# Seven products of a pair in another order, and the last chunk's output with tokens on the partitions

## The chip, the core and the metric

The kernel runs on one core of one Trainium2 chip. The metric is the time of one execution on the device in microseconds; given are the median and the single times. The profile is that of one execution, taken by the hardware profiler. Its engines are called PE (TensorE, matmuls; PEld are its weight loads), DVE (VectorE), ACT (ScalarE), POOL (GpSimd) and SP (SyncE, which issues all DMAs here).

## The reference

One decoder layer over a prompt of 4096 tokens of width 1024, and beside it over 8 single sample tokens, all in float32:

```
h = rmsnorm(x) @ w_in          # u_pool | z_pool | q | k | v | z_attn | g_pool | g_attn
pooled = trailing means of u_pool over 2/4/8/16 tokens, minus u_pool
att    = sliding-window (128) attention, 8 query heads, 2 kv heads, bias and sinks
br_pool = (pooled @ w_grp * pool_scale * silu(z_pool)) @ w_br_pool
br_attn = (att * silu(z_attn)) @ w_br_attn
x = x + (sigmoid(g_pool) * br_pool + sigmoid(g_attn) * br_attn) @ w_out
y = rmsnorm(x, g_final)
```

Outputs are y for prompt and samples, and the keys, values and pooling inputs of the last positions.

## The kernel before

**Numbers.** [...]

**Chunks.** The prompt is worked on in 8 chunks of 512 tokens; chunk 1 carries the 8 sample tokens too. Activations stand with channels on the partitions and tokens along the free dimension. For each chunk the order is: the k and v pair, two pairs of q, the z_attn pair; eight half-blocks, each of which does one pair of the projection and half a block of attention (scores, exponentials, transposes, product with v) in between; the rest of the gate pairs; eight `branch` steps (two products of 4 k-tiles over 512 columns, multiplied by the gates and summed into `mh` and `ml`); eight output steps with `w_out` (24 matmuls of 512 columns each, L938 adds the residual); and in the meantime the normalised input of the next chunk (`prep_sq`, `prep_rs`, `prep_xt`), written into `xt7`. The final norm of a chunk, `finish`, is done during the next chunk's first pairs; after the last chunk it stands alone at the end.

**Pairs.** Two output tiles of the projection (128 rows each) times 512 tokens over 1024 channels are done as a 2x2 block product in the Winograd form of Strassen's scheme: seven products of 4 k-tiles (12 matmuls of 256 columns), instead of eight. `xt7` holds seven combinations of the input, T_1 to T_4 and B_11, B_21, B_22. The weights s1 to s4 are sums of weight blocks, made in chunk 0, kept in DRAM split already, and loaded as 512 KB (L173); 11, 12 and 22 are plain blocks, loaded as 256 KB (L151) and split each time. The partial sums lie in two PSUM banks: Q holds the halves q6 and q1, R the halves r5 and r7. In chunk 1, with 260 columns, the four have a bank each. Products go into q6 (s2), q1 (11, then 12), r5 (s1, then s4), r7 (s3, then 22); between the rounds, copies and additions by ACT and DVE read the banks:

- L300 copies q1 into u2, L301 adds q6 to it
- L305 and L306 add r5 and r7 to u2 into q[3]
- L313 copies q1 into q[0] after product 12
- L317 (chunk 1: L320, L321) adds u2 to r5 and r7 after s4 and 22

A product that writes a bank waits until the readers of that bank are through. `part1` is the first four products, `part2` the other three; in the half-blocks attention stands between them. PSUM has five buffers for pairs, scores and other products together, two for transposes and small things, and one for the product with v.

**Order.** The program is written in the order above; a planner then puts each engine's instructions into one sequence by its own model of times, ready ones first, in the order of the program where several are ready. Each engine works through its sequence in order, and SP's sequence is the order of the DMAs. Weights have 8 split tiles (5 in chunk 0) and 4 raw tiles.

**The end of the last chunk.** Step 7 adds the residual (L938), ACT squares (L947), PE sums the squares over the channels for each token (L382, columns of one), DVE and POOL make 1/rms (L371, L373), PE spreads it over the partitions (L398), ACT copies it (L401), DVE and POOL multiply the eight tiles (L654, L652), and SP stores eight tiles of 256 KB (L657).

## Time and profile before

| what | value |
|---|---|
| median of 2 runs | 2419.95 us (2416.96 and 2422.94) |
| profiled execution | 2424.16 us, span 2422.4 us |
| PE busy | 2336.5 us, 96% |
| DVE busy | 1650.7 us, 68% |
| ACT busy | 1159.9 us, 48% |
| POOL busy | 309.4 us, 13% |
| DMA | 584.67 MB, mean 241 GB/s |

Rows that begin with two numbers are in order of time: start and length in microseconds, engine, line, operation, output and inputs, and in brackets how long the engine had been idle and what ended that. Rows of groups have the number of instructions behind x, then busy microseconds and mean nanoseconds of one, then the idle time before them. Rows of waits have who waited for whom, the total, how often, and the longest.

### The profile page before, as it was taken

To read this page: it belongs to the slowest core of one execution; us is meant where nothing else is said; L and a number is where in the kernel's file an instruction comes from. 1 tells how busy PE (TensorE), PEld (TensorE's weight loads), DVE (VectorE), ACT (ScalarE), POOL (GpSimd) and SP (SyncE) were. 2 spreads that over 40 slices of the span, in tenths; PEclk is the share of its full clock that TensorE was granted. 3 is DMA by queue.
4 is the path that set the end of the run, shared out by engine and by line. 5 is a ranking of instruction groups with operands and counts; after the bars stand their busy time and mean duration, and the time that the engine had idled before them with its cause. 6 is when DMAs were issued, how large, how long until landed. Compare 5 with 4: busy or idle time off the path is not lost.

```text
span 2422.4 us, 44090 instructions
## 1 busy us (share of the span) xinstructions
PE 2336.5 (96%) x16547; PEld 2174.9 (90%) x16547; DVE 1650.7 (68%) x3224; ACT 1159.9 (48%) x2359; POOL 309.4 (13%) x258
## 2 busy tenths in 40 slices
PE   7989999999999999999999999999999999999998
PEld 6979879999999988998889988899889998899986
DVE  7888886856768656676567855677556765668652
ACT  6667545554346633465235642456423663245531
POOL 0000002300024000330004200041001410023000
PEclk9989999999999999999999999999999999999999
DMA  6657878766886667867678667776677776687654
GB/s 215 222 183 252 283 274 305 221 231 235 275 296 237 232 227 244 287 234 238 216 254 280 233 232 233 258 275 227 226 236 270 252 239 220 227 290 244 213 195 144
DMA packets 236515, 584.67 MB, mean 241 GB/s; under 512 B 36828, under 2 KB 39165, under 8 KB 236301
## 3 DMA queue, kind: packets, MB, share of 16 engines
q1 hardware_dynamic: 236300, 581.85, 70.4%
q8 instruction: 131, 2.15, 0.4%
q14 instruction: 84, 0.68, 0.1%
HBM read 517.35 MB, written 64.40 MB: 240 GB/s over the span
## 4 chain that ended last, share of the span: by engine, by line
PE 69%; DVE 15%; DMA 8%; ACT 4%; issue 3%; SPq 0%; POOL 0%; DVEq 0%; ACTq 0%; POOLq 0%
PE hb L184 12%; PE hb L185 12%; PE hb L186 12%; PE mm L184 9%; PE mm L186 9%; PE mm L185 9%; DMA H<-in_xt 3%; DMA wr<-in_xq 2%; DVE w L139 2%; PE tp L521 2%; DMA wr<-in_wall 2%; PE pv L532 2%; DVE H L763 1%; DVE xt L189 1%; DVE oy L654 1%
## 5 line engine op out<-in xcount | busy, mean ns | idle before, releaser
L184 PE MATMUL hb<-xt,w 128*128 128x256 f32 x3312 | 938.7, 284 | 35.2 <-DVE H L306 22.7
L186 PE MATMUL hb<-xt,w 128*128 128x256 f32 x3312 | 931.1, 282 | 5.7 <-DVE w L139 5.6
L185 PE MATMUL hb<-xt,w 128*128 128x256 f32 x3312 | 933.4, 282 | 0.6 <-DVE xt L189 0.3
L184 PEld LDWEIGHTS hb<-xt,w 128*128 128x128 f32 x3312 | 626.5, 189 | 47.0 <-DVE H L306 27.7
L186 PEld LDWEIGHTS hb<-xt,w 128*128 128x128 f32 x3312 | 627.7, 190 | 8.0 <-DVE w L139 8.0
L185 PEld LDWEIGHTS hb<-xt,w 128*128 128x128 f32 x3312 | 626.4, 189 | 3.9 <-DVE xt L189 1.8
L138 ACT CAST w<-wr 128x512 fp32r<-128x512 f32 x586 | 359.2, 617 | 338.4 <-PE hb L186 205.2
L139 DVE TENSOR_TENSOR w<-wr,w 128x512 fp32r<-128x512 f32 x418 | 285.7, 689 | 150.3 <-ACT w L138 147.1
L139 POOL TENSOR_TENSOR w<-wr,w 128x512 fp32r<-128x512 f32 x168 | 253.3, 1510 | 479.7 <-ACT w L138 375.7
L184 PE MATMUL mm<-mh,w 128*128 128x512 f32 (+1 forms) x576 | 213.3, 371 | 1.4 <-ACT mh L898 1.4
L186 PE MATMUL mm<-mh,w 128*128 128x512 f32 (+1 forms) x576 | 213.0, 370 | 1.6 <-DVE w L139 1.6
L185 PE MATMUL mm<-ml,w 128*128 128x512 f32 (+1 forms) x576 | 212.1, 368 | 0.8 <-DVE ml L899 0.6
L373 POOL TENSOR_TENSOR rs<-rs,nhalf 128x4 f32<-128x4 f32 (+1 forms) x18 | 18.4, 1024 | 1341.1 <-DVE rs L371 1341.1
L891 DVE SCALAR_TENSOR_TENSOR H<-H,mm 128x512 f32<-128x512 f32 (+1 forms) x144 | 90.2, 627 | 108.4 <-PE mm L186 107.9
L502 ACT ACTIVATE LL<-LL,nm 128x257 f32<-128x257 f32 (+1 forms) x256 | 126.5, 497 | 68.3 <-DVE nm L499 68.2
L459 ACT CAST xt<-H 128x256 fp32r<-128x256 f32 (+6 forms) x92 | 63.1, 687 | 161.6 <-DVE H L448 111.3
L184 PE MATMUL mm<-xt,w 128*128 128x260 f32 x476 | 135.6, 285 | 0.9 <-ACT U L300 0.5
L185 PE MATMUL mm<-xt,w 128*128 128x260 f32 x476 | 134.7, 283 | 0.7 <-DVE xt L189 0.7
L186 PE MATMUL mm<-xt,w 128*128 128x260 f32 x476 | 134.4, 283 | 0.6 <-DVE w L139 0.3
L186 PEld LDWEIGHTS mm<-mh,w 128*128 128x128 f32 x576 | 108.1, 188 | 22.8 <-DVE w L139 2.5
L185 PEld LDWEIGHTS mm<-ml,w 128*128 128x128 f32 x576 | 108.2, 188 | 21.7 <-DVE ml L899 1.9
L184 PEld LDWEIGHTS mm<-mh,w 128*128 128x128 f32 x576 | 108.1, 188 | 21.0 <-ACT mh L898 1.9
(194 smaller groups left out, 4048.5 us busy)
## 6 DMA issues: line engine op xcount, KB each, us to landing
w<-ss SPq DMA_DIRECT2D x476, 512.0 KB
wr<-in_wall SPq DMA_DIRECT2D x597, 256.0 KB
w<-so SPq DMA_DIRECT2D x96, 512.0 KB
ss<-w SPq DMA_DIRECT2D x56, 512.0 KB
H<-in_xt SPq DMA_DIRECT2D x32, 512.0 KB
wr<-in_xq SPq DMA_DIRECT2D x56, 256.0 KB
H<-in_xt SPq DMA_DIRECT2D x56, 256.0 KB
out_y<-oy SPq DMA_DIRECT2D x28, 512.0 KB
```

What stands on the lines that cost most here:

```text
L138: nc.scalar.copy(w[:, 0], raw)
L139: (eng or nc.vector).tensor_tensor(out=w[:, 1], in0=raw, in1=w[:, 0].bitcast(F32), op=ALU.subtract)
L184: mm(ps, lhsT=w[:, 0, k0 + k, :], rhs=rh, start=start and k == 0, stop=False, **kw)
L185: mm(ps, lhsT=w[:, 0, k0 + k, :], rhs=rl, start=False, stop=False, **kw)
L186: mm(ps, lhsT=w[:, 1, k0 + k, :], rhs=rh, start=False, stop=stop and k == nk - 1, **kw)
L189: nc.vector.tensor_tensor(out=out, in0=a, in1=hi.bitcast(F32), op=ALU.subtract)
L459: nc.scalar.copy(hi[:, s_], x)
L502: nc.scalar.activation(out=L[:, j, k0:2 * P + 1], in_=L[:, j, k0:2 * P + 1], func=AF.Exp, bias=nm[:, j:j + 1], accum_out=den[:, j:j + 1])
L521: nc.tensor.transpose(tp[:, j, :], L[:, j, kb * P:(kb + 1) * P], ident)
L532: mm(pv, lhsT=vs[:, b + kb, g, :], rhs=pt[:, kb, m].rearrange("p j q -> p (j q)"), start=n == 0 and m == 0, stop=n == len(kbs) - 1 and m == 1)
L654: nc.vector.scalar_tensor_tensor(out=y, in0=y, scalar=gf[:, e:e + 1], in1=rsp[:, 0:n], op0=ALU.mult, op1=ALU.mult)
L891: nc.vector.scalar_tensor_tensor(out=t[:, a:b], in0=t[:, a:b], scalar=1.0, in1=ps, op0=ALU.add, op1=ALU.mult)
```

## The change

**The pair.** The order of the products becomes s1, s3 (bank R), s2, 11 (bank Q), s4, 22 (R), 12 (Q), in all chunks. After s3, ACT copies r5 into q[3] and DVE adds r7; after 11, u2 is made as before; after 22, q[3] gets u2 added, and then r5 and r7 get it as before; the copy of q1 into q[0] comes at the end. In chunk 0, s1 came first already. Three k/v, q and u pairs of chunk 0 use another form (`eight1`, `eight2`, `by_rows`) and stay.

```
 def part1(self):
-            if self.c == 0:
-                self.prod(self.r5, "s1", T_1, True)
+            self.prod(self.r5, "s1", T_1, True)
+            self.prod(self.r7, "s3", T_3, not one)
+            nc.scalar.copy(self.q[3], self.r5)
+            nc.vector.tensor_tensor(out=self.q[3], in0=self.r7, in1=self.q[3], op=ALU.add)
             self.prod(self.q6, "s2", T_2, True)
             self.prod(self.q1, "11", B_11, not one)
             nc.scalar.copy(u2, self.q1)
             nc.vector.tensor_tensor(out=u2, in0=self.q6, in1=u2, op=ALU.add)
-            if self.c:
-                self.prod(self.r5, "s1", T_1, True)
-            self.prod(self.r7, "s3", T_3, not one)
-            nc.vector.tensor_tensor(out=self.q[3], in0=self.r5, in1=u2, op=ALU.add)
-            nc.vector.tensor_tensor(out=self.q[3], in0=self.r7, in1=self.q[3], op=ALU.add)
 def part2(self):
-            self.prod(self.q1, "12", B_21, False)
-            nc.scalar.copy(self.q[0], self.q1)
             self.prod(self.r5, "s4", B_22, False)
             self.prod(self.r7, "22", T_4, False)
+            nc.vector.tensor_tensor(out=self.q[3], in0=self.q[3], in1=u2, op=ALU.add)
             ...
+            self.prod(self.q1, "12", B_21, False)
+            nc.scalar.copy(self.q[0], self.q1)
```

**The last chunk's output.** In chunk 7, while branches 4 to 7 run, `wout` loads `w_out` as rows by input channel (sixteen loads of 256 KB) and splits it into the space of `xt7`, which the last gate pair has left (the last eighth goes into two weight tiles). Then `out_tok` replaces the eight output steps and `finish`: for each of four blocks of 128 tokens, `mh` and `ml` are the stationary operand and `w_out` the moving one, 2 x 24 matmuls of 512 columns, so that tokens lie on the partitions. The sum of squares over the channels comes out of ACT's Square, g_final is multiplied along the free dimension, and each block is scaled and stored as soon as it is done. That output goes to a DRAM tensor of its own, `yl`; `finish` and `rstd_tok` lose their branches for the last chunk.

```
+    def out_tok(c, wol, mh, ml):
+        gfb = flat(pair_tile())[:, 0:D]     # g_final on all partitions, one DMA
+        ...
+        for b in range(NB):
+            s = slice(b * P, (b + 1) * P)
+            xr = flat(pair_tile())[:, 0:D]
+            nc.sync.dma_start(out=xr, in_=i["xq"][c, b])
+            ...
+            for e in range(2):
+                n = slice(e * T, (e + 1) * T)
+                ps = ps_mm(T)
+                for k in range(KT):
+                    r = wol[k][e]
+                    h_, l_ = mh[k // 4][:, k % 4, s], ml[k // 4][:, k % 4, s]
+                    mm(ps, lhsT=h_, rhs=r[:, 0], start=k == 0, stop=False)
+                    mm(ps, lhsT=h_, rhs=r[:, 1], start=False, stop=False)
+                    mm(ps, lhsT=l_, rhs=r[:, 0], start=False, stop=k == KT - 1)
+                nc.vector.tensor_tensor(out=y[:, n], in0=ps, in1=xr[:, n], op=ALU.add)
+                nc.scalar.activation(out=xr[:, n], in_=y[:, n], func=AF.Square, accum_out=ss[:, ...])
+                nc.vector.tensor_tensor(out=y[:, n], in0=y[:, n], in1=gfb[:, n], op=ALU.mult)
+            rs = st([P, 8], "rs", 3)
+            nc.vector.tensor_tensor(out=rs[:, 0:1], in0=ss[...], in1=ss[...], op=ALU.add)
+            power(rs, rs, P, 0, 1)
+            nc.vector.tensor_scalar(out=y[:, 0:T], in0=y[:, 0:T], scalar1=rs[:, 0:1], ...)
+            nc.sync.dma_start(out=o["yl"][b][:, 0:T], in_=y[:, 0:T])
+            nc.scalar.activation(out=y[:, T:D], in_=y[:, T:D], func=AF.Identity, scale=rs[:, 0:1])
+            nc.sync.dma_start(out=o["yl"][b][:, T:D], in_=y[:, T:D])
 ...
+            if nxt is None and j > 3:
+                wol += [wout(k) for k in (2 * j - 8, 2 * j - 7)]
 ...
+        if nxt is None:
+            out_tok(c, wol, mh, ml)
+            break
```

## The prediction

> **What bounds the kernel now.** I read the page first, then the waits of TensorE (PE), longest first, then the stretches where they fall.

> ```profile
> span 2422.4 us, 44090 instructions
> ...
> PE 2336.5 (96%) x16547; PEld 2174.9 (90%) x16547; DVE 1650.7 (68%) x3224; ACT 1159.9 (48%) x2359; POOL 309.4 (13%) x258
> ```

> PE is busy for 96% of the span, and the change leaves its matmuls in number and width as they are, apart from the little ones of the last normalisation. So there are two things to win: gaps between matmuls, and the time after the last matmul. The gaps, as engine, line, releaser, then microseconds in total, times, longest:

> ```profile
> PE hb L184 <- DVE H L306: 22.7, 20, 3.0
> ...
> PE hb L184 <- ACT xt L459: 5.7, 6, 1.5
> ...
> PE hb L184 <- DVE U L301: 2.9, 4, 1.2
> ...
> PE S L490 <- DVE U L301: 1.3, 1, 1.3
> ```

> The first row is the one the pair order aims at: product s4 (into r5) waits until L306, the second addition into q[3], has read bank R. The third row is product 12 waiting for bank Q. What such a wait costs, and where the 20 are (PE's order of time: start, length, and in brackets the idle time before):

> ```profile
> 2157.81 0.28 PE L184 MATMUL hb<-xt,w 128*128 128x256 f32 x1
> ...
> 2158.52 0.28 PE L184 MATMUL hb<-xt,w 128*128 128x256 f32 x1
> ...
> 2160.64 0.38 PE L184 MATMUL hb<-xt,w 128*128 128x256 f32 x1 [1.62 <-DVE H L306]
> ```

> ```profile
> 700.89 0.39 PE L184 MATMUL hb<-xt,w 128*128 128x256 f32 x1 [0.30 <-DVE H L306]
> 763.38 0.38 PE L184 MATMUL hb<-xt,w 128*128 128x256 f32 x1 [0.80 <-DVE H L306]
> 847.95 0.39 PE L184 MATMUL hb<-xt,w 128*128 128x256 f32 x1 [1.33 <-DVE H L306]
> 2016.55 0.38 PE L184 MATMUL hb<-xt,w 128*128 128x256 f32 x1 [2.99 <-DVE H L306]
> 2223.48 0.38 PE L184 MATMUL hb<-xt,w 128*128 128x256 f32 x1 [0.77 <-DVE H L306]
> ```

> Six matmuls take 2158.52 - 2157.81 = 0.71 us, so one takes 0.118 and a product of twelve 1.4. Three more after 2158.52 would have let s4 start at 2158.87; it starts at 2160.64. The loss is 1.77 where the record shows 1.62 idle, 0.15 more. The first row is therefore worth 22.7 + 20 x 0.15 = 25.7 us. The waits come back in every chunk of some 292 us at the same places. Place A, the z_attn pair while the chunk before is being normalised: six, 700.89 to 2160.64, together 9.2. Place B, the pair behind the pooling sums: six, 763.38 to 2223.48, together 5.6. Place C, in the branch stage of chunks 2 to 6: five, 847.95 to 2016.55, together 9.6. Three more of about 0.5 make 1.4.

> **The pair order, part by part.** Why L306 is late, at A, B and C (DVE and ACT in order of time):

> ```profile
> 2153.73 2.47 DVE L686 SCALAR_TENSOR_TENSOR q<-H,q 64x1024 fp32r<-64x1024 f32 x2
> 2156.23 0.43 DVE L301 TENSOR_TENSOR U<-hb,U 128x256 f32<-128x256 f32 x1
> 2156.57 2.00 DVE L654 SCALAR_TENSOR_TENSOR oy<-oy,gf,rsb 128x512 f32<-128x512 f32 x2
> 2158.49 0.41 DVE L305 TENSOR_TENSOR H<-hb,U 128x256 f32<-128x256 f32 x1
> 2158.82 1.43 DVE L654 SCALAR_TENSOR_TENSOR oy<-oy,gf,rsb 128x512 f32<-128x512 f32 x1
> 2160.17 0.41 DVE L306 TENSOR_TENSOR H<-hb,H 128x256 f32<-128x256 f32 x1
> ```

> ```profile
> 2219.20 0.42 DVE L301 TENSOR_TENSOR U<-hb,U 128x256 f32<-128x256 f32 x1
> ...
> 2223.03 0.40 DVE L306 TENSOR_TENSOR H<-hb,H 128x256 f32<-128x256 f32 x1
> ```

> ```profile
> 2013.75 0.63 ACT L421 ACTIVATE wr<-wr 128x512 f32<-128x512 f32 x1 [2.94 <-DMA wr<-in_xq]
> ```

> ```profile
> 2015.01 0.69 DVE L139 TENSOR_TENSOR w<-wr,w 128x512 fp32r<-128x512 f32 x1 [3.32 <-ACT w L138]
> ```

> Before, bank R is done with s3 as the fourth product and has only product 12, 1.4 us, until s4; and three DVE operations stand in a row (L301, L305, L306). After, s1 and s3 come first, s2 and 11 stand between them and s4 (2.8 us), and s4 needs one ACT copy and one DVE addition. Each bank now has two products of cover.

> *At A* the queue is full of other work. Four products from 2151.4 on end at 2157.0. The new addition can run when L686 is through, at 2156.2, and end at 2156.7: no wait, unless final-norm multiplies (L654, 0.7 to 1.4 each) are put before it. I take two thirds of 9.2: 6.2. *At B* the addition's input is there by the time L301 now runs, 3.8 us ahead of L306: 5.0 of 5.6. *At C* a late load holds ACT, ACT holds the DVE subtraction L139, and L306 is stuck behind. The first addition will mostly be over by then, but the copy and addition that free bank Q for product 12 fall into the same hole; I take half of 9.6: 4.8. Of the small ones 1. Sum **17 us**; bounds 0 and 25.7.

> What the order adds:

> ```profile
> L300 ACT COPY U<-hb 128x256 f32<-128x256 f32 x116 | 42.4, 365 | 26.9 <-PE hb L186 26.4
> ...
> L455 DVE TENSOR_TENSOR H<-H,H 128x256 f32<-128x256 f32 (+1 forms) x56 | 23.5, 420 | 0.2
> ```

> One more ACT copy of a half tile in each pair: 133 pairs (116 of these, 17 in chunk 1) by 0.365 = 49 us on an engine that is busy 1160 of 2422; hidden under the two products behind it, 0 on the path. DVE keeps four operations; the one that read PSUM (L305) becomes an addition of two SBUF tiles at 0.42, no change. The loads of s1, s3 and s2 now follow one another in SP's queue, 1.5 MB; at the 380 GB/s that the last stores reach (quoted below) that is 4.1 us for three products of 1.4; no PE wait above is on a DMA and eight weight tiles stand ahead, so 0.

> The price is on bank Q: 11 ends part1, so the sum into u2 comes late. In the eight half-blocks that holds up product 12 (behind s4, 22: cover 2.8 us) and, in chunk 1, where a pair takes four of five buffers, the second scores tile, which needs q6's buffer and has one such wait of 1.3 now. These waits (2.9 + 1.3, five in all) may vanish or go to 1.3 in each of eight half-blocks, 10; I take **5 us** more, half way, since one of eight shows it now. [...]

> Pairs: 17 - 5 = **12 us** won.

> **The last chunk, part by part.** The chain behind the last matmul, and the stores:

> ```profile
> 2407.10 0.24 PE mm L186
> ...
> 2407.37 0.70 DVE oy L938
> ...
> 2408.09 0.64 ACT H L947
> ...
> 2409.86 0.17 DVE rs L371
> ...
> 2410.10 1.02 POOL rs L373
> ...
> 2412.94 0.75 DVE oy L654
> ```

> ```profile
> 2414.28 4.41 SPq L657 DMA_DIRECT2D out_y<-oy  x8
> ```

> ```profile
> GB/s 0 0 0 0 22 0 11 0 0 0 0 0 0 0 0 0 0 0 0 0 0 0 0 0 0 0 57 380 374 388 388 404 393 380 44 0 0 0 0 0
> ```

> From 2407.37 to the end at 2422.38 are 15.0 us. The first y is ready at 2412.94 + 0.75 = 2413.7; of the 8.7 us behind it 2.1 MB at 385 GB/s take 5.4, the rest is 3.3. After, only one half block is left: addition 0.70, Square 0.64 (its sum needs about 0.2 more), the g_final multiply in place, which must wait for Square, 0.70, two small DVE operations of 0.17, POOL 1.02 with some 0.1 around it, and a scaling of 512 columns at 0.70, with the other half on ACT: 4.2 us. Then two stores, 0.52 MB, 1.4 us, and the same 3.3: 8.9. Won **6.1 us**; 5 if a lone store is slow, 7 if the small addition goes ahead of the multiply. Four row sums, transposes and a copy leave the path with it.

> What moves ahead of it: sixteen loads of w_out (256 KB, in SP's queue among the branch weights), each with a split, into the free xT space.

> ```profile
> L138 ACT CAST w<-wr 128x512 fp32r<-128x512 f32 x586 | 359.2, 617 | 338.4 <-PE hb L186 205.2 <-PE mm L186 84.4 <-DMA wr<-in_wall 25.8
> L139 DVE TENSOR_TENSOR w<-wr,w 128x512 fp32r<-128x512 f32 x418 | 285.7, 689 | 150.3 <-ACT w L138 147.1
> ```

> ```profile
> 2340.00:2362.40 22.40, 22.40 (x100) 18.22 (x99) 10.81 (x16) 3.58 (x5) 0.00 (x0) 1.00 0.48 165
> ```

> The row is the stretch of the last four branches (PE, PEld, DVE, ACT, POOL busy). ACT gets 16 x 0.617 = 9.9 on top of 3.6, DVE 16 x 0.689 = 11.0 on top of 10.8: 21.8 of 22.4, nearly full. The first output group asks for its eighth weight only after 21 matmuls of 512 columns (L186 in the chain above), 21 x 0.24 = 5 us, so it fits, with no room for an unlucky order; 0 to 4, I take **1 us** lost. DMA moves 4.2 MB there, 187 GB/s, and sixteen 512 KB loads go away behind it. The new residual and g_final loads (2.6 MB) stand behind them, ahead of 45 us of matmuls: 0. Per block, at the durations above, DVE and ACT have some 3.8 and 2.3 us of work in 11: 0.

> **The sum.** 12 + 6.1 - 1 = 17 us. The profiled execution took 2424.2 (its span 2422.4 and 1.8 around it): 2407. The median of the two runs, 2419.95, lies 4.2 lower, so **2403 us**. That is 0.7%; 2%, 48 us, is about what a measurement of this kernel can tell from no change, and all gaps on L306 and L301 with the tail make only 37.

> **Rivals.** *The wait only moves.* DVE does the same work at A, B and C; if it is DVE's backlog that counts, 12 waits for u2 where s4 waited for L306. For it: L654 and L763 stand between the additions. Against: s4 needs one operation instead of three. Tail alone, 6.1 - 1: **2415**. *All gone*, also the L301 waits: 25.7 + 4.9 + 6.1: **2383**. For it: one product more (1.4) and two operations fewer in front (0.8) exceed every L306 loss but the one of 3.1. Against: place C.

> *Slower: the new copy stands behind the exponentials.* Before, L305 read bank R by itself; after, the addition must wait for ACT's copy, and in a half-block ACT is tied up at a stretch:

> ```profile
> 2214.09 2.10 ACT LL L502 x8
> ```

> ```profile
> ACT LL L502 <- DVE nm L499: 68.2, 47, 3.7
> ```

> With 68.2 / 47 = 1.5 of waiting for their input, 2.1 of exponentials, copy 0.37 and addition 0.42, bank R comes free 4.4 us after s3, against 2.8 of cover: 1.6 lost. It decides the sign from eleven half-blocks on (17 / 1.6) of 64; with half of them, 51 - 17 = 34 more: **2454**. [...] Against it: the copy can be asked for once s1 is done, well ahead of these exponentials.

> *It does not shorten the tail* (w_out's splits stop PE as long as the tail gains): 2403 + 6 = 2409, inside the forecast.

> **How the numbers follow.** Forecast 2392 to 2411: 0.5. Wait moves, 2411 to 2422: 0.2. All gone, 2378 to 2392: 0.13. Slower, 2422 to 2460 and beyond: 0.17, of which 0.04 over 2468. Range 2380 to 2432, which leaves out the far half of the slow case and a little of the fast one. Faster by over 2%: 0.02; within: 0.94; slower: 0.04.

> **What would show it.** Right: PE's waits on the addition that frees R fall below 9 us; at most 10 on the one into u2; 9 us from last matmul to end, with two stores there; no PE wait on the w_out splits over 1. Wrong: a PE wait on the new copy in every half-block, or DVE idle for ACT in front of its addition; then the slow case holds.

## The result, and the profile after

The changed kernel takes 2391.4 us, the median of two runs (2390.6 and 2392.1), against 2419.95 before: 28.6 us less, ratio 0.9877 with a 95% interval of 0.9857 to 0.9897. It is faster beyond doubt and by less than 2%. The forecast was 2403, 17 us less. Two runs of each are few: beside the later experiments the kernel before had medians of 2424.9 to 2426.2 us over 7 to 23 runs and the changed kernel 2391.7 over four (ratio 0.9862), so the difference is nearer 33 us. The profiled execution took 2392.1 (span 2390.3), so against its own forecast of 2407 the trace is 15 us ahead.

The page of the changed kernel, its span and engines:

```profile
span 2390.3 us, 44003 instructions
...
PE 2331.3 (98%) x16527; PEld 2170.6 (91%) x16527; DVE 1660.0 (69%) x3247; ACT 1211.5 (51%) x2520; POOL 298.4 (12%) x259
```

To see where the time went I cut both spans at the same two points of the work, ACT's first copy of the keys in chunk 2 and in chunk 7. The rows are the first two chunks, chunks 2 to 6, and the last chunk with the end (length, then busy time of PE, PEld, DVE, ACT, POOL, granted clock, DMA share, GB/s). Stretches of before:

```profile
0.00:670.40 670.40, 625.75 (x4597) 589.88 (x4598) 513.40 (x1039) 360.75 (x742) 52.56 (x60) 0.98 0.72 246
670.40:2130.90 1460.50, 1433.72 (x10025) 1328.44 (x10025) 965.17 (x1856) 679.03 (x1377) 213.96 (x166) 1.00 0.72 244
2130.90:2422.40 291.50, 277.00 (x1929) 256.60 (x1927) 172.10 (x329) 120.09 (x242) 42.88 (x32) 0.98 0.63 216
```

And after:

```profile
0.00:668.80 668.80, 626.84 (x4594) 590.22 (x4595) 509.99 (x1039) 369.46 (x774) 54.92 (x60) 0.98 0.73 246
668.80:2107.30 1438.50, 1429.63 (x10025) 1326.33 (x10025) 968.45 (x1856) 705.19 (x1462) 202.45 (x166) 1.00 0.72 248
2107.30:2390.30 283.00, 274.85 (x1913) 254.08 (x1911) 181.55 (x352) 136.81 (x286) 41.03 (x33) 0.99 0.60 209
```

Of the 32.1 us of span, 1.6 come from the first two chunks, 22.0 from chunks 2 to 6 (4.4 each) and 8.5 from the last. In the middle row PE's idle time, length minus busy, falls from 26.8 to 8.9, and PE is busy for 99.4% of that stretch. PE's waits after, the rows that answer to those of before and the new ones (total, times, longest):

```profile
PE hb L184 <- ACT w L138: 6.3, 3, 3.6
PE mm L186 <- DVE w L139: 5.9, 2, 5.6
PE hb L184 <- DVE U L303: 4.5, 5, 1.5
...
PE mm L832 <- DVE mx L488: 2.7, 4, 0.7
...
PE mm L833 <- DVE ypl L189: 1.6, 4, 0.4
PE hb L184 <- DVE H L299: 1.4, 3, 0.5
...
PE hb L184 <- ACT xt L452: 0.5, 1, 0.5
```

L299 is the addition that now frees bank R: PE waits for it 1.4 us in three waits, where it waited for L306 22.7 in twenty. L303 is the sum into u2 (L301 before). The waits on xT at the beginning of a chunk (L452, before L459) went from 5.7 to 0.5, the waits of the pooled products (L832, L833) are new, and so is one of 5.6 us on a split weight. (Split: each float32 operand is kept as a high part, for weights ACT's copy at L138, and the rest that is left when that is subtracted, L139; a product of two is three matmuls, high x high, high x rest and rest x high, L184 to L186.)

Place A after, the z_attn pair of chunk 7 (DVE in order of time):

```profile
2131.93 1.41 DVE L642 SCALAR_TENSOR_TENSOR oy<-oy,gf,rsb 128x512 f32<-128x512 f32 x2
2133.27 0.42 DVE L299 TENSOR_TENSOR H<-hb,H 128x256 f32<-128x256 f32 x1
2133.60 2.26 DVE L642 SCALAR_TENSOR_TENSOR oy<-oy,gf,rsb 128x512 f32<-128x512 f32 x2
2135.78 0.41 DVE L303 TENSOR_TENSOR U<-hb,U 128x256 f32<-128x256 f32 x1
```

The final-norm multiplies (L642) do stand ahead of the addition, but it ends at 2133.7, and u2, made after product 11, ends 2.5 us later. Bank R is free while s2 and 11 still run.

The chain behind the last matmul, and the two stores:

```profile
2382.60 0.25 PE mm L683
...
2382.87 0.70 DVE ot L684
...
2383.59 0.73 ACT H L685 x2
...
2384.35 0.69 DVE ot L686
...
2385.14 0.16 DVE rs L369
...
2385.41 0.58 POOLq L1057
...
2386.02 0.72 ACT ot L693
```

```profile
2386.53 0.33 SPq L692 DMA_DIRECT2D out_yl<-ot  x1
2386.96 0.38 SPq L694 DMA_DIRECT2D out_yl<-ot  x1
```

From 2382.85 to 2390.3 are 7.5 us, of 15.0 before. The chain takes 3.9, and from the issue of the last store to the end are 3.3.

### The profile page after: what moved, and what is told of

Same layout as the page of the kernel before. It is cut to its first block, busy times and chain, and to the rows that moved or that the text cites. A ratio compares the mean times of both kernels' runs of the same rounds, so it can differ in the third digit from the quotient of the medians.

```text
span 2390.3 us, 44003 instructions
## 1 busy us (share of the span) xinstructions
PE 2331.3 (98%) x16527; PEld 2170.6 (91%) x16527; DVE 1660.0 (69%) x3247; ACT 1211.5 (51%) x2520; POOL 298.4 (12%) x259
## 4 chain that ended last, share of the span: by engine, by line
PE 74%; DVE 14%; DMA 5%; ACT 4%; issue 2%; SPq 1%; POOL 0%; DVEq 0%; POOLq 0%; ACTq 0%
PE hb L186 13%; PE hb L184 13%; PE hb L185 13%; PE mm L186 9%; PE mm L184 9%; PE mm L185 9%; DMA wr<-in_wall 2%; DVE H L796 2%; DVE w L139 2%; DMA H<-in_xt 2%; PE pv L525 2%; PE tp L514 2%; DVE LL L488 1%; ACT LL L495 1%; DVE PT L189 1%
## 5 line engine op out<-in xcount | busy, mean ns | idle before, releaser
L184 PE MATMUL hb<-xt,w 128*128 128x256 f32 x3312 | 934.9, 283 | 13.3 <-ACT w L138 6.3
L186 PE MATMUL hb<-xt,w 128*128 128x256 f32 x3312 | 931.8, 282 | 4.3 <-DVE w L139 4.0
L184 PEld LDWEIGHTS hb<-xt,w 128*128 128x128 f32 x3312 | 626.1, 189 | 20.5 <-ACT w L138 8.2
L186 PEld LDWEIGHTS hb<-xt,w 128*128 128x128 f32 x3312 | 626.8, 189 | 8.0 <-DVE w L139 7.7
L138 ACT CAST w<-wr 128x512 fp32r<-128x512 f32 x588 | 363.1, 620 | 336.0 <-PE hb L186 134.5
L139 DVE TENSOR_TENSOR w<-wr,w 128x512 fp32r<-128x512 f32 x420 | 287.6, 690 | 129.0 <-ACT w L138 115.4
L139 POOL TENSOR_TENSOR w<-wr,w 128x512 fp32r<-128x512 f32 x168 | 248.2, 1486 | 513.1 <-ACT w L138 418.9
L186 PE MATMUL mm<-mh,w 128*128 128x512 f32 (+1 forms) x512 | 188.5, 369 | 5.9 <-DVE w L139 5.9
L184 PE MATMUL mm<-mh,w 128*128 128x512 f32 (+1 forms) x512 | 189.1, 370 | 2.0 <-ACT mh L931 1.1
L185 PE MATMUL mm<-ml,w 128*128 128x512 f32 (+1 forms) x512 | 187.7, 367 | 0.6 <-DVE ml L932 0.6
L371 POOL TENSOR_TENSOR rs<-rs,nhalf 128x4 f32<-128x4 f32 (+2 forms) x21 | 18.6, 885 | 1316.3 <-DVE rs L369 1195.7
L452 ACT CAST xt<-H 128x256 fp32r<-128x256 f32 (+6 forms) x92 | 63.1, 687 | 150.8 <-DVE H L441 109.0
L184 PE MATMUL mm<-xt,w 128*128 128x260 f32 x476 | 135.2, 284 | 0.0
L186 PE MATMUL mm<-xt,w 128*128 128x260 f32 x476 | 134.6, 283 | 0.0
L186 PEld LDWEIGHTS mm<-mh,w 128*128 128x128 f32 x512 | 96.6, 189 | 24.4 <-DVE w L139 6.8
L184 PEld LDWEIGHTS mm<-mh,w 128*128 128x128 f32 x512 | 96.6, 189 | 20.2 <-ACT mh L931 2.0
L185 PEld LDWEIGHTS mm<-ml,w 128*128 128x128 f32 x512 | 96.6, 189 | 18.4 <-DVE ml L932 1.2
```

The lines of the kernel that those rows point to most:

```text
L138: nc.scalar.copy(w[:, 0], raw)
L139: (eng or nc.vector).tensor_tensor(out=w[:, 1], in0=raw, in1=w[:, 0].bitcast(F32), op=ALU.subtract)
L184: mm(ps, lhsT=w[:, 0, k0 + k, :], rhs=rh, start=start and k == 0, stop=False, **kw)
L185: mm(ps, lhsT=w[:, 0, k0 + k, :], rhs=rl, start=False, stop=False, **kw)
L186: mm(ps, lhsT=w[:, 1, k0 + k, :], rhs=rh, start=False, stop=stop and k == nk - 1, **kw)
L452: nc.scalar.copy(hi[:, s_], x)
```

## The experiments

The kernel before, run beside these, had medians of 2424.9, 2426.2 and 2425.2 us in the three groups of runs; ratios are to that.

**The pair order alone.** The last chunk is that of before.

```
 part1 and part2 of the changed kernel; all else as in the kernel before
```

> Pair order alone, the last chunk as before. If the two parts add up: the tail stays at 15.0 us from the last matmul to the end, PE's waits on the addition that frees bank R go from 22.7 to under 2 us, and the time is that of the whole change plus the 7.5 us that its tail lost, 2399 us. If part of the gain came from the planner placing everything anew (the waits at chunk starts on the new xT, 5.7 us to 0.5), it can come out some 6 us higher, 2405.

Measured: 2397.4 us, ratio 0.9886 (0.9866 to 0.9905). Its end behind the last matmul is the old one, 14.7 us. The stretch of chunks 2 to 6:

```profile
665.70:2104.00 1438.30, 1429.09 (x10025) 1326.30 (x10024) 969.08 (x1856) 706.12 (x1461) 202.85 (x166) 1.00 0.73 248
```

The middle chunks are those of the changed kernel to 0.2 us: all of the 22 us comes with the pair's new order and its early copy.

**The last chunk's output alone.**

```
 part1 and part2 of the kernel before; all else as in the changed kernel
```

> The last chunk's output alone, pairs in the old order. Adding up: 22.7 us of PE waits on the second addition stay, the tail takes 7.5 us instead of 15.0, no new PE wait from the w_out splits: 2412 us. If those splits, or a new plan of the loads before them, cost PE time, 2416 or more.

Measured: 2415.9 us, 9.0 less than the kernel before beside it, ratio 0.9961 (0.9946 to 0.9976), 7.6 us behind the last matmul.

```profile
PE hb L184 <- DVE H L306: 22.1, 22, 2.6
...
PE hb L184 <- ACT xt L454: 4.1, 6, 1.5
```

The waits of the old order are all there. The two parts bring 1.14% and 0.39%, together 1.53%; both at once brought 1.23% (1.03 to 1.43) and, in a later repetition, 1.38% (1.22 to 1.55). The interval of the sum overlaps both, so they add as far as these runs can tell.

**The old order with the new way of emptying bank R.** This parts cover from work: s4 still comes one product after s3, but fewer operations stand in front of it.

```
-            nc.vector.tensor_tensor(out=self.q[3], in0=self.r5, in1=u2, op=ALU.add)
+            nc.scalar.copy(self.q[3], self.r5)
             nc.vector.tensor_tensor(out=self.q[3], in0=self.r7, in1=self.q[3], op=ALU.add)
 ...         # behind product 22
+            nc.vector.tensor_tensor(out=self.q[3], in0=self.q[3], in1=u2, op=ALU.add)
```

> Old order of the products (s2, 11, s1, s3, 12, s4, 22) and old tail, but bank R is read as after: ACT copies r5, DVE adds r7 at once, and u2 is added later. So R comes free after one DVE operation that needs no u2, with one product (1.4 us) of cover as before. If the order is what counts (two products of cover), most of the waits stay: 12 us or more on that addition, 2410 us or more. If the fewer operations in front are what counts, they go under 5 us and the time is that of the pair order alone, near 2399.

Measured: 2431.1 us, ratio 1.0024 (1.0009 to 1.0040), slower than before.

```profile
667.90:2132.20 1464.30, 1439.06 (x10026) 1334.54 (x10025) 961.58 (x1856) 699.98 (x1462) 210.10 (x166) 1.00 0.73 244
```

```profile
PE hb L184 <- DVE H L306: 22.9, 22, 2.3
```

The wait is as long as before (22.7). That fewer operations stand in front of s4 gains nothing by itself. At place A of chunk 4 ACT's copy of r5 was done at 1276.73, but DVE came to the addition only at 1279.19, behind three final-norm multiplies that had begun at 1275.61; at 17 of the 22 waits DVE went straight from other work into the addition, and at five it had stood idle for ACT's copy.

**The new order with the old way of emptying bank R.** The counterpart: s2 and 11 stand between, but R can be read only once u2 exists, so the cover is gone.

```
             self.prod(self.r5, "s1", T_1, True)
             self.prod(self.r7, "s3", T_3, not one)
-            nc.scalar.copy(self.q[3], self.r5)
-            nc.vector.tensor_tensor(out=self.q[3], in0=self.r7, in1=self.q[3], op=ALU.add)
 ...         # behind the sum into u2
+            nc.vector.tensor_tensor(out=self.q[3], in0=self.r5, in1=u2, op=ALU.add)
+            nc.vector.tensor_tensor(out=self.q[3], in0=self.r7, in1=self.q[3], op=ALU.add)
```

> The changed kernel without the early copy: bank R is read as before, after u2 is there, so with the new order s4 follows 11 with no product of cover, behind one ACT copy and three DVE operations (0.37 + 3 x 0.42 and hand-overs, 1.8 us). If cover between the rounds is what counts, PE waits 1.8 us in each of the some 70 pairs without attention in between: 125 us more, 2516. If the planner puts other matmuls into the hole, less than 30 more, 2420.

Measured: 2440.2 us, ratio 1.0048 (1.0032 to 1.0063).

```profile
PE hb L184 <- ACT w L138: 13.2, 10, 3.6
...
PE hb L184 <- DVE U L301: 12.2, 16, 1.2
PE hb L184 <- DMA w<-ss: 6.7, 7, 1.7
...
PE hb L184 <- DVE H L303: 3.6, 10, 0.4
```

```profile
0.00:686.20 686.20, 632.76 (x4604) 593.22 (x4605) 513.55 (x1039) 361.14 (x742) 54.52 (x60) 0.98 0.72 240
686.20:2145.60 1459.40, 1440.27 (x10025) 1328.98 (x10024) 949.85 (x1857) 680.68 (x1377) 195.79 (x166) 1.00 0.73 245
```

Neither theory had this in between. The planner puts other matmuls where s4 would wait, so the wait on R itself is small (L303, 3.6); what it pulls forward then waits for its weights and for u2. The middle chunks are where they were before (1459.4 of 1460.5), the first two 16 us longer, and that although this run has the new output of the last chunk, which alone won 9 us. Order and early copy work only together: each alone is slower than before, by 0.2 and 0.5%. Each edit also gets a new plan, and no run separates the cover from the plan that goes with it; that the cover itself is at work can be seen at single places, such as place A in the section on the result.

**A second copy of r5.** ACT gets the new copy twice in each pair; if it is on the path, that shows.

```
             nc.scalar.copy(self.q[3], self.r5)
+            nc.scalar.copy(self.q[3], self.r5)
```

> The changed kernel with the new ACT copy of r5 made twice in each pair: 133 x 0.37 = 49 us more on ACT. If two products of cover hide it, 2391 us, within 3. If the copy is on the path in the half-blocks (the slow rival of the prediction), 64 x 0.37 = 24 us more, 2415.

Measured: 2397.7 us, ratio 0.9890 (0.9869 to 0.9911). ACT is busy 1252.1 us instead of 1211.5.

```profile
PE hb L184 <- DVE U L304: 4.8, 6, 1.0
...
PE hb L184 <- DVE H L300: 2.0, 6, 0.4
```

ACT has 41 us more to do, and the time is 2397.7 against 2391 to 2392, with overlapping intervals of the ratio: some 6 us, more than the 3 that were expected of a hidden copy, and far from the 24 of a copy on the path. The wait on bank R went from 1.4 to 2.0; PE's waits for the pooled products went from 4.3 (2.7 and 1.6) to 8.2 (5.0 and 3.2). On bank R the copy is hidden, and the slow rival, which lived on it, is out.

**The waits on xT.** They went away without having been aimed at. If a late load of x (`in_xt`) in SP's queue makes them, loads that POOL issues should take them from the kernel before.

```
-                nc.sync.dma_start(out=xt[:, e, 0:T], in_=i["xt"][c, :, kk + 4 * e, :])
+                nc.gpsimd.dma_start(out=xt[:, e, 0:T], in_=i["xt"][c, :, kk + 4 * e, :])
```

> The kernel before, with the loads of the next chunk's x (L443) issued by POOL instead of SP. If the PE waits at the chunk starts (on the new xT, 5.7 us in six) come from these loads standing in SP's queue behind weight loads that wait for a free tile, the waits fall under 1 us and the time by 6 us, ratio to before 0.9975. If they come from the product that a chunk begins with (s2 before, s1 after), they stay, and so does the time.

Measured: 2430.8 us, ratio 1.0016 (1.0000 to 1.0032), no gain.

```profile
PE mm L184 <- ACT mh L898: 5.2, 5, 2.5
...
PE hb L185 <- DVE xt L189: 2.8, 5, 0.9
```

The wait on ACT's copy of xT is down to one of 0.6 us, but its successor, the rest that DVE makes, is waited for five times, and new waits stand in the branches. The run left the other loads of x (`in_xq`) with SP, and ACT's waits on those stayed: 68.9 us, 66.8 before, 20 to 24 in every run with the new order. What in the new order takes the 5 us away is not settled. All runs in the new order of products have one such wait after the first chunk's, of 0.4 to 1.9 us (two, of 0.9 and 0.8, in the run with both edits of chunk 0 below); all in the old order with the loads as they were have five or six.

**The hole in chunk 0.** The changed kernel has one wait of 5.6 us that the kernel before does not have. The run with the old order and the early copy has one of 5.8 us at the same stage, and the one with the new order and the old copy one of 5.3, so either half of the edit is enough to bring it. Two ways to close it: the old order in chunk 0 alone, or the stores of the combined weights off SP's queue. Both runs, and the two after them, also put the last half block's g_final multiply behind the two small operations of the norm.

```
             if self.c == 0:
                 return self.old1()      # part1 as before; part2 likewise
```

> The changed kernel with two edits: the pairs of chunk 0 in the old order (there the changed kernel has a new PE wait of 5.6 us in its output steps, and 4.3 us at half the granted clock behind it), and for the very last half block the g_final multiply moved behind the small additions of the norm, beside POOL. If the new order in chunk 0 brings that wait, it goes: 5.6 + 2.0 us; the tail falls from 7.5 to 6.8 us; together 2383 us, ratio to before 0.984. If the wait belongs to the plan of the output steps whatever the pair order, it stays: 2390.

```
-            nc.sync.dma_start(out=cache[key][:, 0], in_=hi.bitcast(F32))
-            nc.sync.dma_start(out=cache[key][:, 1], in_=low)
+            nc.gpsimd.dma_start(out=cache[key][:, 0], in_=hi.bitcast(F32))
+            nc.gpsimd.dma_start(out=cache[key][:, 1], in_=low)
```

> The changed kernel with the same edit at the tail, and the stores of the combined weights in chunk 0 (L358, L359) issued by POOL instead of SP; the new pair order in all chunks. If the wait of 5.6 us in chunk 0 comes from w_out's raw loads standing in SP's queue behind these stores, which wait for their sums, it goes: 2383 us, ratio to before 0.984. If DVE's own work in front of the split is the cause, it stays: 2390.

Measured: 2395.9 us, ratio 0.9863 (0.9848 to 0.9877), and 2394.8, ratio 0.9862 (0.9848 to 0.9876). Neither reached the 2383 expected, and both ratios are that of the changed kernel repeated (0.9862, below). With the old order in chunk 0, PE has a new wait in chunk 1:

```profile
PE S L515 <- DVE U L305: 5.1, 1, 5.1
```

With the stores issued by POOL:

```profile
PE mm L184 <- ACT mh L934: 6.9, 3, 4.5
...
PE mm L186 <- DVE w L139: 2.1, 1, 2.1
```

The hole is gone in the first and down to 2.1 us in the second, and each time another of 4.5 to 5.1 us opened. Then both together, the multiply alone, and the changed kernel once more:

> The changed kernel with both edits of chunk 0 that missed alone (the old order of products in chunk 0; the two stores of each combined weight issued by POOL) and the multiply of the last half block moved. Each closed one hole in chunks 0 and 1 and opened another. If the holes come from SP's queue in two different ways, both together close them: chunks 0 and 1 together at 622 us or less (633 in the changed kernel), and 2383 to 2387 us. If a hole is only the sign that weights are being combined, loaded and split at the limit there, it comes up at yet another place: chunks 0 and 1 together at 630 to 636 us, and 2391 to 2397 us.

> The changed kernel, with the g_final multiply of the very last half block behind the two small operations of the norm, so that its 0.70 us leaves the chain behind the last matmul. In the two runs that had this edit beside another one the end was 7.2 us instead of 7.5. If the chain counts: 0.3 to 0.7 us below the unaltered changed kernel of this call, which no timing here can tell from nothing; if the plan of chunk 0 changes with it: up to 4 us either way.

> The changed kernel unaltered, so that the two below have their own comparison. Ratio to the kernel before 0.987 +- 0.002, some 2393 to 2396 us if the kernel before is again at 2425; end behind the last matmul 7.5 us.

Measured: both together 2400.2 us, ratio 0.9891 (0.9875 to 0.9907); the multiply alone 2389.3, 0.9853 (0.9834 to 0.9871); the changed kernel again 2391.7, 0.9862 (0.9845 to 0.9878). First two chunks with the multiply alone, then in the repetition:

```profile
0.00:665.00 665.00, 622.37 (x4594) 586.01 (x4595) 509.80 (x1039) 369.33 (x774) 53.89 (x60) 0.98 0.74 248
```

```profile
0.00:668.30 668.30, 624.03 (x4594) 587.58 (x4595) 509.98 (x1039) 369.29 (x773) 54.06 (x60) 0.98 0.74 246
```

Both edits together don't close the holes, as the second theory had it, though 2400.2 us lies above the 2391 to 2397 that it gave. And the last two kernels have the same sequence of instructions there, yet differ by 3.3 us: the first two chunks scatter by that much, and a few microseconds won or lost there by an edit can't be told from it. The multiply itself shortens the end from 7.5 to 7.4 us; its ratio overlaps that of the unaltered kernel, so none of these versions is shown to be faster than it.

## Why the prediction was right and where it was not

**The mechanism held.** The waits on the addition that frees bank R were foreseen to fall below 9 us and fell to 1.4; the first sign of the slow rival, PE waiting for the new copy in every half-block, is not there. The second sign that was named for it, DVE idle for ACT in front of its addition, is there, 41 times:

```profile
DVE H L299 <- ACT H L298: 45.1, 41, 2.0
```

The slow case does not hold all the same, since PE lost 1.4 us on that addition: DVE idle shows only that the copy comes late, not that the cover is used up, so this sign was badly chosen. What bank R gave in the middle chunks, 22.5 us, needs the new order and the early copy together, as the runs with one without the other show. The rival that the wait only moves fell as a whole, but not everywhere, as place B shows.

The number is less good than the mechanism. 2391.4 lies just below the forecast's own interval, 2392 to 2411, in the one that the rival "all gone" had with a chance of 0.13; and that rival's account is not what happened, since the waits on u2 stayed and place B won nothing. Two effects that were in no sum, 5.4 won on xT and 5.6 lost at B, cancel, and that is luck.

**The terms that were mis-sized.** Pairs: I had 17 won on L306 and 5 lost on u2. Counted from start to start of the matmuls, the eighteen waits of before in chunks 2 to 6 were worth 23.1, and 0.6 is left there.

- *Places A and C*: I took 6.2 of 9.2 and 4.8 of 9.6; all of it went. At A the final-norm multiplies do get ahead of the addition and it is still in time. At C I assumed that the late load would stay and bank Q's readers would fall into it. ACT waits much less for that load; its waits on it were, before,

```profile
ACT wr L421 <- DMA wr<-in_xq: 66.8, 38, 5.4
```

and after,

```profile
ACT wr L414 <- DMA wr<-in_xq: 20.0, 22, 2.5
```

The old order with the shorter way out of bank R still has 54.7, and the new order with the old way 21.7, so it goes with the order; by what step of the plan, I haven't shown.

- *Place B*: I took 5.0 of 5.6. Here the wait did move (PE behind the pooling sums of chunk 2, after):

```profile
762.12 0.38 PE L184 MATMUL hb<-xt,w 128*128 128x256 f32 x1 [0.91 <-DVE U L303]
764.45 0.50 PE L833 MATMUL mm<-ypl,w 128*128 128x512 f32 x1 [0.42 <-DVE ypl L189]
765.85 0.50 PE L832 MATMUL mm<-yph,w 128*128 128x512 f32 x1 [0.67 <-DVE mx L488]
```

Bank R costs PE 0.4 us at two of the six places. At three others product 12 waits for u2, as in the first row (0.91, 0.63 and 0.55 us), the way the rival had it. And then the pooled products wait for DVE, which is busy for 9.96 of the 10.0 us from 757 to 767: four times two waits, 5.6 us with what they cost behind them. Place B won nothing.

- *u2*: 5 more was taken; PE's waits on it went from 2.9 + 1.3 to 4.5 + 0.4, 0.7 more. Product 12 writes q1's half alone, and still it waited for DVE's addition that reads q6's half of the bank (L301, 2.9 in four waits before; L303, 0.91 at 762.12 after), not for ACT's copy of q1 into u2.

- *Not foreseen*: the waits on xT, worth 5.4 in chunks 2 to 6, are gone. Their row stands in the prediction, but no term of the sum was made of it. The first product of a chunk was s2, which reads T_2, and is s1 now, which reads T_1; that is the edit that could matter, but no run separates it.

For chunks 2 to 6: 23.1 - 0.6 on bank R, + 5.4 on xT, - 1.8 on u2, - 5.6 at B make 20.5 of 22.0. The rest is in small pieces: three new waits, 1.5 together, and 2.9 won in pieces of 0.1 us, mostly the second matmul after a stall, which starts late too: at 2160.64 of before it comes 0.22 us behind the first, where the ones after it come 0.12 apart.

**The end.** Forecast 8.9, measured 7.5. The chain was sized at 4.2 and took 3.9, since POOL's power is on one column now instead of four and takes 0.58 with its start, where I carried over 1.02 (in the changed kernel four on 128x1 take 0.55 each, fifteen on 128x4 1.01). (The terms that I listed make 4.4 if the two small operations take 0.17 each; they took 0.24 together.) Behind the chain I put 4.7, 1.4 of transfer and then 3.3; 3.6 are left, from 2386.74 to the end. The transfer is still there: the bytes of both stores move from 2387.37 to 2388.81, and 1.5 us follow. What shrank is the start. The first store is issued at 2386.53, while ACT still scales the second half, and so the bytes begin to move 0.6 us behind the chain; before, they began 1.4 us behind the first finished y (2413.69 to 2415.13). The splits of w_out were put at 1 us lost; PE waits for none of them: 0.

**The last chunk** held the remaining 25.7 - 23.1 = 2.6 of the loss on L306, the two waits of 1.62 and 0.77 at 2160.64 and 2223.48; one of 0.4 us is left. Of the 8.5 us that the last stretch gained, the end makes 7.5 and only 1.0 lies ahead of it; where the other microsecond of bank R's went, no run shows.

**Chunks 0 and 1** had no wait on L306 to lose. They gained 1.6 in the profiled pair of runs, a new hole in chunk 0 included, whose size stands below; by the experiments that figure has a scatter of some 3 us, so it shows nothing.

**The median.** The forecast took 4.2 off because the profiled execution of before lay above the median of two; that of after lies 0.8 above its median. Of the 15 us between 2407 and 2392, 3.4 are given back that way, and 11.6 remain between 2403 and 2391.4. By the later medians of before, 2424.9 to 2426.2, its profiled execution, 2424.2, was an ordinary one, and the 4.2 came from two runs that happened to be short.

## What to carry to other kernels

Where products alternate between two banks, count for each bank the products that stand between its last write and its next one, and see that its reader can start without the other bank's result: here either alone made the kernel slower (ratios 1.0024 and 1.0048), both together took away nearly all of the waits (22.7 us to 1.4). Waits on a backlogged engine went whole (places A and C) or came back at the next instructions (place B): the fractions that I took were wrong at all three places, and the question to ask of each is whether the next instruction there needs the same engine. And a plan that moved closed and opened holes of some microseconds here in places that the edit wasn't aimed at (5.4 us won on xT, a hole of 5.6 in chunk 0); the three attempts made here to close them gained nothing that could be measured.

## What the hardware showed

One wait of PE cost more than its length. Stretches around the hole of chunk 0, after:

```profile
326.00:333.00 7.00, 6.23 (x26) 4.72 (x26) 6.75 (x11) 4.97 (x8) 0.66 (x2) 1.00 0.72 226
333.00:339.60 6.60, 0.99 (x4) 0.30 (x2) 5.92 (x13) 3.29 (x7) 0.50 (x1) 0.80 0.97 337
339.60:343.90 4.30, 4.26 (x10) 3.40 (x11) 4.15 (x6) 0.47 (x1) 1.79 (x2) 0.51 0.65 227
343.90:348.00 4.10, 4.10 (x19) 3.30 (x19) 2.05 (x3) 1.57 (x3) 0.00 (x0) 1.00 0.59 178
```

```profile
2016.50:2020.00 3.50, 3.45 (x27) 3.35 (x28) 0.99 (x3) 0.00 (x0) 1.38 (x1) 1.00 0.91 310
```

The run with the pair order alone has such a hole in the same stage, 5.4 us on a split weight:

```profile
329.00:334.80 5.80, 0.49 (x3) 0.06 (x1) 5.24 (x12) 2.57 (x6) 0.48 (x2) 0.77 0.96 336
334.80:339.00 4.20, 4.14 (x10) 3.27 (x11) 4.20 (x8) 1.11 (x2) 0.66 (x2) 0.50 0.60 209
339.00:343.00 4.00, 4.00 (x19) 3.22 (x18) 1.96 (x3) 0.75 (x2) 0.00 (x0) 1.00 0.67 194
```

What brings the clock down and up again, no run here separates.
